# Low parts of the mixers' weight pieces: all on VectorE, in place of VectorE and GpSimd in turns

## The chip, the core and the metric

The kernel runs on one core of a Trainium2 chip. The metric is the device time of one execution in microseconds, the median of several runs. All times inside the execution come from one run that was taken with the hardware profiler; they count from the start of that run's span.

## What is computed

One layer of a streaming encoder on a sequence of 512 frames of width 1024, in float32:

```python
x = x + 0.5 * swiglu(rms_norm(x, norm_ffn1), gate1, up1, down1)     # D_FF = 2816
p = rms_norm(x, norm_mix) @ w_in
q, k, v, rw = split(p)                                              # two mixers share one projection
o_sb = rms_norm(stick_breaking_attention(q, k, v))                  # 8 heads of 64, causal
o_rw = rwkv7_time_mix(rw, ...)                                      # 8 heads, a recurrence over 512 steps
x = x + concat(o_sb, o_rw) @ w_out
x = x + 0.5 * swiglu(rms_norm(x, norm_ffn2), gate2, up2, down2)
```

The mixers are the three middle lines of work: the input projection, the attention, the recurrence and the output projection.

## The kernel before, in words

The kernel has three stages: the first feed-forward layer (to about 355 us), the mixers (to about 755 us) and the second feed-forward layer. Every weight is read once from HBM, in pieces of 128 x 512 floats.

**How a piece is made ready.** A float32 product is built from three faster ones: each operand is written as a high part plus a low part, and `mm3` (L183) issues high x high, high x low and low x high into one PSUM bank. `load` (L155) takes one of three `raw` slots and puts a load of 256 KB on SP's queue. `w_split` (L160) then has two steps: ScalarE copies the piece, rounded, into the high part (L163), and the engine handed in as `pool` subtracts, low = raw - high (L164). The high and the low part have three slots each as well. A `raw` slot comes free when L164 has read it, so L164 also sets when the load three pieces on can start.

**Which engine subtracts.** `load_split` (L167) chooses it. Outside the mixers it is VectorE. A flag is set before the mixers and cleared after them, and while it is set a counter sends the odd pieces to GpSimd:

```python
wct[0] += 1
pool = nc.gpsimd if mixing[0] and wct[0] % 2 else nc.vector
```

The mixers have 76 such pieces: 28 of `wrw` (keys, receptances, values and small factors of the recurrence) and 16 of `wqk`, all called `w` in the trace, 16 of `wv` (for `sv`, the attention's values) and 16 of `wo` (the output projection). In turns, that is 38 for each engine.

**What else VectorE and GpSimd do there.** VectorE empties PSUM banks, builds the operands of the recurrence (`item_r`, L598 to L627: `AR` at L608 to L610, `kkn` at L621, two quarters of `BK` at L625), runs a forward substitution of 15 short steps (`G` and `H`, L706 and L708), sums the attention's scores (`l` and `r`, L871 to L873) and adds the output projection into `x` (L917). GpSimd makes the other two quarters of `BK` (L625), a few masks and identities, and the sum of squares of the two inner norms (L219). It cannot read PSUM.

**What sets the order.** The program is written out flat. A loop by hand at the end of the mixers deals out three kinds of side work (the substitution and block inverse `I`, the chain of states `C`, the attention `T`) between the steps of the dense stream, by a table of costs, and gives `I` and `C` a higher priority. From these priorities, the dependencies and the free slots the framework's scheduler fixes, when the program is built, one order of instructions for each engine, by durations of its own for each engine and operation. At run time each engine works down its own list; an instruction that has to wait holds up all that stand behind it. Which engine an instruction is put on is an input of that scheduler, so a change of engine can also change the order elsewhere.

Of the kernel before, what the change touches and what calls it, by code (L numbers as in the profile page):

```python
# [82 lines left out]
def layer(ctx, tc, a, out, dbg=None):  # L83
    nc = tc.nc
# [3 lines left out]
    pd = ctx.enter_context(tc.tile_pool(name="pd", bufs=1, space=bass.MemoryType.DRAM))  # L88
    pp = ctx.enter_context(tc.tile_pool(name="pp", bufs=1, space=bass.MemoryType.PSUM))
    uid = [0]  # L90
    mixing = [False]

    def nm(s):
        uid[0] += 1
# [7 lines left out]
    def slot(tag, s="t", dt=F32, shape=None):  # L102
        return pb.tile(shape or [P, T], dt, tag="s" + tag, name=nm(s), bufs=NB[tag])
# [46 lines left out]
        return cst[:, CST[n][0]:CST[n][1]]  # L150


    wct = [0]

    def load(src, n, s="w"):  # L155
        raw = pw.tile([P, T], F32, tag="raw", name=nm(s), bufs=NW)
        nc.sync.dma_start(raw[:, :n], src)
        return raw

    def w_split(raw, n=T, s="w", pool=nc.vector, cp=nc.scalar.copy):  # L160
        hi = pw.tile([P, T], F32R, tag="whi", name=nm(s + "h"), bufs=NW)
        lo = pw.tile([P, T], F32R, tag="wlo", name=nm(s + "l"), bufs=NW)
        cp(hi[:, :n], raw[:, :n])  # L163
        pool.tensor_tensor(lo[:, :n], raw[:, :n], hi[:, :n].bitcast(F32), SUB)  # L164
        return hi, lo

    def load_split(src, n, s="w", pool=None, cp=nc.scalar.copy):  # L167
        if pool is None:
            wct[0] += 1
            pool = nc.gpsimd if mixing[0] and wct[0] % 2 else nc.vector  # L170
        return w_split(load(src, n, s), n, s, pool, cp)

    mms = []
# [69 lines left out]
    def gemm(ps, wsrc, xs, step=lambda: None):  # L243

        n = len(xs)
        for k0 in range(0, n, 4):
            kn = min(4, n - k0)
            wh, wl = load_split(wsrc[:, k0 * P:(k0 + kn) * P], kn * P)
            for k in range(k0, k0 + kn):
                ks = slice((k - k0) * P, (k - k0 + 1) * P)  # L250
                mm3(ps, wh[:, ks], wl[:, ks], xs[k][0], xs[k][1], k == 0, k == n - 1)
            step()
# [113 lines left out]
    def ffn(g, wgu, wd, last):  # L366
# [4 lines left out]
        if last:  # L371
            xsrc = pd.tile([KD, P, T], F32, name="xmid")
            for k in range(KD):
                nc.sync.dma_start(xsrc[k], X[k])
            xs = norm_in(g, XTAG)
            first = None
        else:
            xs = []

            def first():  # L380

                ps = [bank(("acc", "ma")[q], "gu"[q]) for q in range(2)]
                z = slot("f", "warm", BF16)
                nc.vector.memset(z, 0.0)
                for _ in range(11):
                    nc.tensor.matmul(ps[1], lhsT=z[:, 0:P], rhs=z, start=True, stop=True)
                for k in range(KD):
                    if k:
                        nc.sync.dma_start(X[k], a["xT"][k])
                    if k % 4 == 0:  # L390
                        w = [load_split(wgu[q][:, k * P:(k + 4) * P], T, pool=nc.vector,
                                        cp=nc.scalar.copy if k or q else nc.vector.tensor_copy) for q in range(2)]
                    xs.append(split(X[k], XTAG[k], v(g, k), "x"))
                    ks = slice(k % 4 * P, (k % 4 + 1) * P)
                    for q in range(2):
                        mm3(ps[q], w[q][0][:, ks], w[q][1][:, ks], xs[k][0], xs[k][1], k == 0, k == KD - 1)
                nc.sync.dma_start(cst, a["cst"])
                nc.sync.dma_start(lev, a["lev"])
                return ps
# [90 lines left out]
        return  # L490


    mixing[0] = True
    w2a2 = slot("g", "w2a2")
    nc.sync.dma_start(w2a2, a["w2a2"])
    g2 = slot("f", "g2")
# [327 lines left out]
    def item_sv(half):  # L824
        ps2 = [bank("acc", "sv") for _ in range(2)]
        for k in range(KD):
            wh, wl = load_split(a["wv"][k], T, "wv")
            for i in range(2):
                ts_ = slice((2 * half + i) * P, (2 * half + i + 1) * P)
                mm3(ps2[i], xs[k][0][:, ts_], xs[k][1][:, ts_], wh, wl, k == 0, k == KD - 1)  # L830
        yield
        for i in range(2):
            tt = 2 * half + i
            Vt.append(slot("v", "Vt"))
            act(Vt[tt], ps2[i], AF.Copy, scale=rs[:, tt:tt + 1])
# [147 lines left out]
    if dbg == "mix":  # L983
        return

    mixing[0] = False
    wct[0] = 0
    ffn("nf2", a["wgu2"], a["wd2"], True)


# [38 lines left out]
def build(d, dbg=None):  # L1029
    import concourse.bacc as bacc  # L1030
    nc = bacc.Bacc("TRN2", target_bir_lowering=False, num_devices=1)
    a = {n: nc.dram_tensor(n, x.shape, mybir.dt.from_np(x.dtype), kind="ExternalInput").ap() for n, x in d.items()}
    out = nc.dram_tensor("out", (KD, P, T), F32, kind="ExternalOutput").ap()
    with tile.TileContext(nc) as tc, ExitStack() as ctx:
        layer(ctx, tc, a, out, dbg)
    return nc
# [9 lines left out]
```

## Time and profile before

| what | value |
|---|---|
| median of 3 runs | 1126.36 us (1126.17 to 1126.9) |
| the profiled execution's own time | 1128.58 us |
| its span (first to last instruction) | 1126.8 us |
| TensorE (PE) busy | 1093.4 us, 97% |
| VectorE (DVE) busy | 722.2 us, 64% |
| ScalarE (ACT) busy | 522.1 us, 46% |
| GpSimd (POOL) busy | 130.1 us, 12% |
| chain that ended last | PE 78%, DVE 14%, ACT 3%, POOL 1% |

The profile names engines PE, PEld (weight loads of PE), DVE, ACT, POOL and SP. An instruction is given with its line, its operation, the tile it writes and those it reads. "Idle before" is the time for which the engine had nothing running before an instruction, with what ended it. PEclk is the clock granted to TensorE as a share of full speed; it has two levels, 2.4 GHz (1.0) and 1.2 GHz (0.5), and a value between is a mean over the stretch.

### The profile page before, as it was taken

What the parts mean: (1) busy time and instruction counts of PE and PEld (TensorE: products, weight loads), DVE (VectorE), ACT (ScalarE), POOL (GpSimd) and SP (SyncE); (2) the same over time, 40 slices, a digit from 0 to 9 for tenths busy, and PEclk for the clock granted to TensorE, in tenths of its full rate; (3) what the DMA queues carried; (4) which work ended last, traced back from release to release, by engine and by line L of the source; (5) the groups of instructions that cost most, each with busy time, mean ns of one, the idle gap of its engine ahead of it and who ended that gap; (6) DMA issues with size and microseconds to landing.
All of it is one profiled execution on the core that took longest, in us unless ns stands there. A gap on an engine that the chain in (4) does not pass through costs nothing.

```text
span 1126.8 us, 18892 instructions
## 1 busy us (share of the span) xinstructions
PE 1093.4 (97%) x7363; PEld 899.4 (80%) x7363; DVE 722.2 (64%) x1258; ACT 522.1 (46%) x958; POOL 130.1 (12%) x99
## 2 busy tenths in 40 slices
PE   8989999999999999999999998998999999999998
PEld 6789999998888766766667675676889999998887
DVE  6997777763333466477776768577987777753322
ACT  5554545542323563464644644544555454532221
POOL 0100000000003233221311302023100000000000
PEclk9999999999999998999999899999999999999999
DMA  6333333343333223311302112034333333343342
GB/s 196 102 111 96 104 111 105 103 136 96 102 96 95 95 66 108 93 47 35 82 20 57 41 24 57 11 111 131 95 122 100 90 102 113 94 143 114 113 115 67
DMA packets 70698, 104.24 MB, mean 93 GB/s; under 512 B 19664, under 2 KB 21840, under 8 KB 70608
## 3 DMA queue, kind: packets, MB, share of 16 engines
q1 hardware_dynamic: 70608, 103.02, 30.9%
q8 instruction: 58, 0.95, 0.4%
q14 instruction: 32, 0.26, 0.1%
HBM read 97.23 MB, written 5.77 MB: 91 GB/s over the span
## 4 chain that ended last, share of the span: by engine, by line
PE 78%; DVE 14%; ACT 3%; issue 2%; DMA 2%; POOL 1%; SPq 0%; DVEq 0%; ACTq 0%; POOLq 0%
PE dn L185 7%; PE dn L184 7%; PE dn L186 7%; PE pa L184 4%; PE pa L186 4%; PE pa L185 4%; PE inv L736 3%; PE g L186 2%; PE g L185 2%; PE g L184 2%; PE pc L186 2%; PE pc L185 2%; PE pc L184 2%; PE u L186 2%; PE u L185 2%
## 5 line engine op out<-in xcount | busy, mean ns | idle before, releaser
L164 DVE TENSOR_TENSOR wl<-w,wh 128x512 fp32r<-128x512 f32 x198 | 135.6, 685 | 196.0 <-ACT wh L163 194.6
L163 ACT CAST wh<-w 128x512 fp32r<-128x512 f32 (+1 forms) x219 | 132.2, 604 | 239.9 <-PE dn L185 153.6
L184 PE MATMUL dn<-hdh,wh 128*128 128x512 f32 x240 | 93.4, 389 | 0.0
L185 PE MATMUL dn<-hdl,wh 128*128 128x512 f32 x240 | 93.4, 389 | 0.0
L186 PE MATMUL dn<-hdh,wl 128*128 128x512 f32 x240 | 93.4, 389 | 0.0
L186 PEld LDWEIGHTS dn<-hdh,wl 128*128 128x128 f32 x240 | 45.1, 188 | 9.4
L184 PEld LDWEIGHTS dn<-hdh,wh 128*128 128x128 f32 x240 | 45.1, 188 | 9.3
L185 PEld LDWEIGHTS dn<-hdl,wh 128*128 128x128 f32 x240 | 45.1, 188 | 9.2
L163 ACT CAST wh<-wg 128x512 fp32r<-128x512 f32 x48 | 29.7, 620 | 38.0 <-PE u L185 21.0
L164 POOL TENSOR_TENSOR wl<-w,wh 128x512 fp32r<-128x512 f32 x22 | 31.2, 1420 | 129.6 <-ACT wh L163 107.5
L184 PE MATMUL dn<-hd,wh 128*128 128x512 f32 x112 | 43.6, 389 | 0.0
L185 PE MATMUL dn<-hd,wh 128*128 128x512 f32 x112 | 43.6, 389 | 0.0
L186 PE MATMUL dn<-hd,wl 128*128 128x512 f32 x112 | 43.6, 389 | 0.0
L186 PE MATMUL u<-xnh,wl 128*128 128x512 f32 x96 | 37.5, 390 | 0.9 <-DVE wl L164 0.9
L184 PE MATMUL g<-xnh,wh 128*128 128x512 f32 x96 | 37.6, 391 | 0.0
L185 PE MATMUL g<-xnl,wh 128*128 128x512 f32 x96 | 37.5, 391 | 0.0
L184 PE MATMUL u<-xnh,wh 128*128 128x512 f32 x96 | 37.5, 390 | 0.0
L185 PE MATMUL u<-xnl,wh 128*128 128x512 f32 x96 | 37.5, 390 | 0.0
L186 PE MATMUL g<-xnh,wl 128*128 128x512 f32 x96 | 37.5, 390 | 0.0
L164 DVE TENSOR_TENSOR wl<-wg,wh 128x512 fp32r<-128x512 f32 x48 | 33.0, 687 | 5.3 <-ACT wh L163 5.3
L318 ACT CAST s3h<-s 128x512 fp32r<-128x512 f32 x24 | 14.9, 620 | 41.3 <-DVE s L316 41.3
L219 POOL TENSOR_TENSOR sq<-sq,sq 128x512 f32<-128x512 f32 x12 | 18.0, 1500 | 111.3 <-ACT sq L135 110.6
(358 smaller groups left out, 3263.8 us busy)
## 6 DMA issues: line engine op xcount, KB each, us to landing
w<-wgu SPq DMA_DIRECT2D x80, 256.0 KB, 2.9
w<-wd SPq DMA_DIRECT2D x80, 256.0 KB, 2.6
wu<-wgu SPq DMA_DIRECT2D x48, 256.0 KB, 2.9
wg<-wgu SPq DMA_DIRECT2D x48, 256.0 KB, 2.5
w<-wrw SPq DMA_DIRECT2D x28, 256.0 KB, 2.8
x<-xT SPq DMA_DIRECT2D x16, 256.0 KB, 5.3
w<-wqk SPq DMA_DIRECT2D x16, 256.0 KB, 2.9
wv<-wv SPq DMA_DIRECT2D x16, 256.0 KB, 2.6
```

Source lines behind the costliest of these rows:

```text
L163: cp(hi[:, :n], raw[:, :n])
L164: pool.tensor_tensor(lo[:, :n], raw[:, :n], hi[:, :n].bitcast(F32), SUB)
L184: mms.append(nc.tensor.matmul(ps, lhsT=lh, rhs=rh, start=start, stop=False, skip_group_check=again))
L185: nc.tensor.matmul(ps, lhsT=lh, rhs=rl, start=False, stop=False, skip_group_check=again)
L186: nc.tensor.matmul(ps, lhsT=ll, rhs=rh, start=False, stop=stop, skip_group_check=again)
L219: (eng if k < KD - 1 else nc.vector).tensor_tensor(tot, tot, sq, ADD)
L318: nc.scalar.copy(hi, t_)
L736: nc.tensor.matmul(ps[rows[p], cc], lhsT=l_[rows[p], cc], rhs=r[rows[p], cc], start=True, stop=True)
```

## The change

In the mixers every low part is made by VectorE. The flag and the counter go, and the choice in `load_split` is always VectorE; nothing else is edited. The other work of GpSimd stays where it is.

```diff
-    mixing = [False]
...
-    wct = [0]
...
     def load_split(src, n, s="w", pool=None, cp=nc.scalar.copy):
         if pool is None:
-            wct[0] += 1
-            pool = nc.gpsimd if mixing[0] and wct[0] % 2 else nc.vector
+            pool = nc.vector
         return w_split(load(src, n, s), n, s, pool, cp)
...
-    mixing[0] = True
     w2a2 = slot("g", "w2a2")
...
-    mixing[0] = False
-    wct[0] = 0
     ffn("nf2", a["wgu2"], a["wd2"], True)
```

## Rows read from the trace of the kernel before

**Rows 1.** Busy time, page: us, share of the span, instructions.
```profile
PE 1093.4 (97%) x7363; PEld 899.4 (80%) x7363; DVE 722.2 (64%) x1258; ACT 522.1 (46%) x958; POOL 130.1 (12%) x99
```

**Rows 2.** Windows: stretch, length, busy of PE, PEld, DVE, ACT, POOL, PEclk, DMA, GB/s.
```profile
360.00:755.00 395.00, 378.23 (x3292) 273.17 (x3291) 262.76 (x495) 199.67 (x376) 94.58 (x74) 0.98 0.22 58
415.00:430.00 15.00, 11.32 (x54) 8.32 (x54) 11.35 (x13) 4.34 (x8) 6.89 (x6) 0.79 0.34 102
430.00:440.00 10.00, 10.00 (x113) 7.77 (x112) 3.53 (x9) 4.80 (x9) 3.95 (x5) 0.97 0.34 87
500.00:510.00 10.00, 9.67 (x73) 5.64 (x71) 9.59 (x12) 6.89 (x15) 5.30 (x4) 1.00 0.09 26
675.00:690.00 15.00, 12.63 (x54) 7.83 (x52) 13.40 (x28) 9.46 (x19) 1.30 (x1) 0.89 0.17 33
```

**Rows 3.** Waits in the mixers: waiter, releaser, us in all, times, longest.
```profile
DVE AR L768 <- PE MG L766: 18.1, 6, 6.9
...
PE wo L184 <- DVE x L917: 3.3, 2, 1.8
...
PE A L659 <- DVE BK L625: 2.7, 2, 1.8
```

**Rows 4.** Groups by line, GpSimd's low parts: count, busy us, mean ns, idle before.
```profile
L164 POOL TENSOR_TENSOR wl<-w,wh 128x512 fp32r<-128x512 f32 x22 | 31.2, 1420 | 129.6 <-ACT wh L163 107.5 <-PE q L186 8.9 <-DMA G<-db 6.9
...
L164 POOL TENSOR_TENSOR wvl<-wv,wvh 128x512 fp32r<-128x512 f32 x8 | 11.4, 1428 | 24.6 <-ACT wvh L163 16.2 <-DVE rn L851 8.2
L164 POOL TENSOR_TENSOR wol<-wo,woh 128x512 fp32r<-128x512 f32 x8 | 10.3, 1286 | 79.2 <-ACT woh L163 71.1 <-DVE H L708 8.1
```

**Rows 5.** Timeline of VectorE: start us, duration us, instruction, idle before it.
```profile
367.77 0.83 DVE L200 SCALAR_TENSOR_TENSOR xl<-x,vec,xh 128x512 fp32r<-128x512 f32 x1 [0.80 <-ACT xh L135]
...
416.57 1.78 DVE L610 TENSOR_TENSOR AR<-xr,Pd 128x512 f32<-128x512 f32 x1
418.27 1.76 DVE L621 TENSOR_TENSOR kkn<-kkn,a 128x512 f32<-128x512 f32 x1
...
422.31 1.75 DVE L625 TENSOR_TENSOR BK<-kkn,Pi 64x512 f32<-64x512 f32 x1
423.99 0.67 DVE L625 TENSOR_TENSOR BK<-kf,Pi 64x512 f32<-64x512 f32 x1
424.59 0.67 DVE L164 TENSOR_TENSOR wvl<-wv,wvh 128x512 fp32r<-128x512 f32 x1
...
442.19 1.16 DVE L706 TENSOR_TENSOR G<-G,H 64x25 f32<-64x25 f32 x1
...
504.77 0.68 DVE L608 SCALAR_TENSOR_TENSOR AR<-kkn,Pd 128x504 f32<-128x504 f32 x1 [0.41 <-ACT Pd L135]
...
735.18 1.42 DVE L197 TENSOR_TENSOR orl<-orw,orh 128x512 fp32r<-128x512 f32 x1 [0.24 <-ACT orh L196]
```

**Rows 6.** Timeline of GpSimd, the same columns.
```profile
417.88 1.61 POOL L164 TENSOR_TENSOR wvl<-wv,wvh 128x512 fp32r<-128x512 f32 x1
420.18 1.66 POOL L625 TENSOR_TENSOR BK<-kkn,Pi 64x512 f32<-64x512 f32 x1 [0.69 <-DVE kkn L621]
421.92 1.60 POOL L164 TENSOR_TENSOR wvl<-wv,wvh 128x512 fp32r<-128x512 f32 x1
...
501.15 1.29 POOL L164 TENSOR_TENSOR wl<-w,wh 128x512 fp32r<-128x512 f32 x1 [11.14 <-ACT wh L163]
```

**Rows 7.** Timeline of TensorE, the same columns.
```profile
419.54 0.50 PE L185 MATMUL sv<-wvl,xh 128*128 128x512 f32 x1 [0.66 <-POOL wvl L164]
...
422.44 0.50 PE L185 MATMUL sv<-wvl,xh 128*128 128x512 f32 x1 [1.25 <-DVE wvl L164]
424.72 0.59 PE L659 MATMUL A<-AR,BK 64*128 64x128 f32 x2 [1.77 <-DVE BK L625]
...
449.45 0.50 PE L185 MATMUL sv<-wvl,xh 128*128 128x512 f32 x1 [0.91 <-DVE wvl L164]
...
680.86 1.10 PE L209 MATMUL qm<-rn,cst 128*128 128x512 f32 x2 [0.53 <-DVE rn L848]
```

## The prediction

> **What bounds the kernel now.** I read the busy times first, then a table by windows, then who waited for whom in the mixers, then the groups by line, and last the timelines of three engines side by side. By the busy times TensorE works for 97% of the span [rows 1]. In the mixers, 360 to 755 us, it is busy for 378.23 of 395 us at a mean clock of 0.98 [rows 2]: 16.8 us stand idle there, and about 8 us (395 x 0.02) are lost to the lower clock. No change on VectorE and GpSimd can win more than these two. VectorE is busy for 262.76 us there, 67% on the mean, but 9.59 of 10 us from 500 to 510 [rows 2]; TensorE's longest waits are for VectorE, those for `x` and `BK` [rows 3] among them, in stretches where VectorE itself has no pause. So the question is what the change does to VectorE in those few stretches, not to the mean. (A measurement of this kernel tells about 0.2%, 2.25 us, from no change.)
>
> **What goes and what comes.** GpSimd loses 22 + 8 + 8 = 38 subtractions with means of 1.29 to 1.43 us [rows 4]. VectorE gets them. The undisturbed one at 424.59 lasts 0.67 us, but its predecessor, just as long, started 0.60 us before it [rows 5], so each takes 0.60 us of VectorE's list: 38 x 0.60 = 22.8 us.
>
> Part of that comes back. While GpSimd runs, a VectorE instruction with two inputs stands still: `kkn` at 418.27 takes 1.76 us beside GpSimd's `wvl` of 417.88, and `BK` at 422.31 takes 1.75 us beside that of 421.92, while the next `BK` takes 0.67 us alone [rows 5, 6]. That is 1.08 us each. Even the tiny `G` step of 25 columns at 442.19 takes 1.16 us [rows 5]. The timeline has 18 VectorE instructions stretched by a low part of GpSimd, the first at 367.77, the last at 735.18 [rows 5]; what they take beyond undisturbed ones of their kind adds up to 11.7 us. VectorE's list thus grows by 22.8 - 11.7 = 11.1 us, from 67 to about 69% of the mixers. The Trainium skill (SBUF — State Buffer, Who interferes with whom) says that the two engines share a pair of ports under an exclusive lock, and that the loser blocks for the whole instruction. If each of the 38 met such an instruction, by that rule, 38 x 1.29 = 49 us would come back, VectorE would get lighter and the loss below would go: the sum would be -3.5 us in place of -2.0. The trace shows the block, but for 18 of 38.
>
> **Place by place.** A moved instruction counts where TensorE's next idle time is ended by VectorE or by the low part itself.
>
> *415 to 425 us.* TensorE waits 0.66, 1.25 and 1.77 us [rows 7], for GpSimd's `wvl`, for VectorE's `wvl` and for `BK`. `AR` at 416.57 [rows 5] waited for GpSimd's own `BK`, which stays. Then the first moved `wvl` runs on VectorE from 418.3 to 418.9, where GpSimd ended it at 419.49 (417.88 + 1.61) [rows 6]: TensorE goes on 0.5 us sooner. `kkn` loses a stall of 1.08 us for an added 0.60 us: 0.5 us. GpSimd's `BK` of 420.18 [rows 6] and VectorE's `wvl` behind it move up with it. The second moved `wvl` replaces the stall of `BK` at 422.31: another 0.5 us. `A` starts 1.0 us sooner: **-1.0**, and 2.7 of the 3.68 us of idle time stay.
>
> *The clock there.* It is 0.79 over 15 us and 0.97 over the next 10 [rows 2]: 15 x 0.21 + 10 x 0.03 = 3.45 us lost. From 675 to 690 us TensorE waited 0.53 us [rows 7] and then 1.8 us for `x` [rows 3], 2.3 us in all, and lost 15 x 0.11 = 1.65 us [rows 2]. With 2.7 us of idle time left the first place comes near the second, so I take 1.65 us for the loss that remains: **-1.8**. Ends: 0, if the fall stays as it is, and -3.45, if it goes.
>
> *438 to 450 us.* Three moved `wvl` add 1.8 us ahead of the one that ends the 0.91 us wait at 449.45 [rows 7]; three stalls of `G` steps (the one shown and two more) give back 2.2 us: **-0.4**.
>
> *690 to 702 us.* Two moved `wol` add 1.2 us, two stretched sums give back 1.6 us, ahead of one of the two waits for `x` [rows 3]. Some of it ends in waits for ScalarE: **-0.3**.
>
> *500 to 635 us.* Five moved instructions (like the one at 501.15 [rows 6]) stand in full stretches of VectorE ahead of waits of TensorE for `BK`, `Z`, states and scores, and no VectorE instruction is stretched by them today. Each costs between 0 us, where a pause as the 0.41 us at 504.77 [rows 5] swallows it, and 0.60 us. I take half: **+1.5**.
>
> *The other 26.* I cost them at nothing: after them TensorE has work in its list, and the pieces stand up to three ahead. The 38 that VectorE makes today show that this cover is thick: TensorE waited for a low part only in the `sv` stages. If the cover went, each would cost 0.60 us less its share of the remaining stalls (11.7 - 2.2 - 2.2 - 1.6 = 5.7 us): 26 x 0.60 - 5.7, some +10 us.
>
> *Queues.* SP's list is the same: 76 loads in the same places of the program. Their slots come free at the subtraction, on GpSimd after its 1.29 us, on VectorE after 0.67 us and whatever stands ahead. What stands ahead can be long: VectorE waits 6.9 us once for a product `MG` [rows 3], and a low part behind that would hold its load as well. On GpSimd the `BK` quarters and masks only get freer.
>
> **Sum.** -1.0 - 1.8 - 0.4 - 0.3 + 1.5 = -2.0 us. The profiled execution took 1128.58 us (span 1126.8) and would take 1126.6; it stands 2.2 us above the median of the runs, so the forecast goes on the median: 1126.36 - 2.0 = **1124.4 us**. Its own range, with the ends of the clock and of the five (0 to +3.0): 1121.2 (-1.7 - 3.45 + 0) to 1127.7 (-1.7 + 0 + 3.0).
>
> **The rivals.** *VectorE becomes the bound in its full stretches* (500 to 520 and 556 to 640 us). For it: 9.59 of 10 us busy [rows 2] with a pause of 0.41 us [rows 5] before the operands of `A`. Price: eight moved instructions there without a stall, 8 x 0.60 = 4.8 us, one more fall of the clock like that at 675 us, 1.65 us, and of the gains only the -1.0 and -0.7 stay: +4.7, about **1131**. It decides once the pauses before `AR` and `Z` are used up, that is when 0.60 us exceeds the 0.41. Against it: in these stretches ScalarE or TensorE ended some of VectorE's pauses, so part is swallowed. The Trainium skill (Perfetto Trace Analysis, Optimizing Scalar/DVE Operations) stands on this side: with VectorE saturated, handing some of its work to GpSimd may pay, though the shared port may eat that up. The trace bears out both halves, the full 10 us and the 18 stalls.
>
> *The places link up.* With the stalls gone at 415 to 425 us the clock doesn't fall there (-3.45) and the five are swallowed (0): -1.7 - 3.45 = -5.2, **1121.2**. For it: if the second moved `wvl` is put behind the `BK` pair in VectorE's list, another 0.60 us goes, and 2.1 us of idle time stay, less than the 2.3 us of the second place. Against: that order is not known.
>
> *It is hidden.* TensorE is busy 378 of 395 us; what is won in one pause is waited for in the next. **1126.4**.
>
> That the change doesn't do what it says I leave out: one argument decides the engine. But the scheduler orders all lists anew, and a shift of a few us either way through other neighbours is in the range.
>
> **How the numbers follow.** Forecast 0.40, places linked 0.22, hidden 0.10, VectorE the bound 0.28. Of the forecast's own range, 1121.2 to 1127.7, I put 0.17 of the 0.40 below 1124.1, the rest within 0.2%. Faster 0.22 + 0.17 = 0.39; same 0.23 + 0.10 = 0.33; slower 0.28. The range for 8 in 10 reaches from below the linked case, 1118.5, to just above the slower one, 1131.5; outside lie the lost cover (+10) and luck of the order.
>
> **What would show it.** GpSimd's busy time falls by 53 us to about 77, with no line of low parts; VectorE's rises by some 14 (38 x 0.67 - 11.7). `kkn` and the first `BK` at 415 to 425 us take 0.67 us; TensorE's waits there add up to 2.7 us or less and the clock of 415 to 430 us is near 0.89. Wrong would be: waits of TensorE for `BK`, `Z` or `x` longer by 0.6 us each, a fall of the clock at a new place, or TensorE waiting for low parts in `k`, `r`, `q` or `wo`.

## The result, and the profile after

The changed kernel takes **1121.83 us** (median of 6 runs, 1120.58 to 1122.28) beside 1127.82 us for the kernel before (6 runs, 1126.17 to 1130.95): a ratio of **0.995, interval 0.9931 to 0.9968**. Run again later it gave 0.9968 (0.9953 to 0.9983). It is faster, by 3.6 to 5.6 us where 2.0 were forecast. The experiments below show that most of this is not the work of the engine that the change names: with the order held, putting the 38 subtractions on VectorE changes the time by -1.4 to +1.9 us (ratios that are each uncertain by about 2 us), while the new order that the scheduler gave the lists wins 4.3 to 4.4 us by itself.

The page of the changed kernel (its profiled execution took 1122.11 us, its span is 1120.3 us; lines stand 2 to 4 lower than before):

```profile
PE 1090.7 (97%) x7363; PEld 896.7 (80%) x7363; DVE 727.5 (65%) x1296; ACT 520.6 (46%) x958; POOL 79.3 (7%) x61
```

GpSimd lost 50.8 us and 38 instructions against [rows 1]; VectorE has the 38 more, and yet is busy for 5.3 us more only. The windows, with the columns of [rows 2]:

```profile
360.00:755.00 395.00, 382.12 (x3319) 275.27 (x3319) 275.11 (x543) 204.39 (x386) 48.42 (x40) 1.00 0.23 63
415.00:430.00 15.00, 12.84 (x86) 9.60 (x86) 11.81 (x20) 5.20 (x10) 3.10 (x2) 1.00 0.48 137
430.00:440.00 10.00, 10.00 (x98) 8.04 (x97) 5.38 (x18) 6.03 (x11) 3.76 (x4) 1.00 0.35 95
500.00:510.00 10.00, 9.07 (x60) 6.25 (x55) 9.60 (x13) 6.96 (x14) 3.95 (x2) 1.00 0.01 2
510.00:580.00 70.00, 68.33 (x732) 49.11 (x731) 47.33 (x104) 33.33 (x69) 8.47 (x8) 1.00 0.19 51
675.00:690.00 15.00, 11.39 (x46) 7.22 (x44) 13.39 (x31) 7.37 (x21) 0.00 (x0) 0.89 0.24 50
```

In the mixers TensorE is busy for 382.12 of 395 us in place of 378.23, and the mean clock rounds to 1.00 in place of 0.98. The window 415 to 430 us runs at full clock, 675 to 690 us does not. One window that I had not read before the change is the most telling later on; the same 510 to 580 us of the kernel before:

```profile
510.00:580.00 70.00, 65.90 (x665) 47.37 (x667) 48.20 (x102) 36.55 (x74) 15.53 (x13) 1.00 0.19 51
```

TensorE's waits in the mixers of the changed kernel (waiter, releaser, us in all, times, longest):

```profile
PE z L857 <- DVE rn L847: 3.3, 1, 3.3
PE wT L876 <- DVE r L869: 2.9, 6, 0.9
PE inv L732 <- DVE Z L738: 2.0, 4, 0.7
PE sv L182 <- DVE wvl L162: 1.5, 1, 1.5
PE A L655 <- DVE BA L658: 0.5, 1, 0.5
...
PE wo L181 <- DVE x L913: 0.4, 2, 0.3
```

TensorE's two waits of [rows 3] changed: `wo` waits for `x` for 0.4 us, not 3.3, and `A` for `BK` not at all, where it was 2.7. A new one came, 3.3 us of `z` for `rn` at 675 to 679 us, and the one fall of the clock that is left in the mixers (680.0 to 683.4 us) stands behind it. Before, the granted clock fell to its lower level from 423.8 to 430.7, 635.5 to 642.3 and 686.7 to 690.1 us. The last product of the mixers ends at 756.4 us, not 763.4: all of the gain lies in the mixers, and they start within 0.1 us of each other.

At the first place of the prediction, VectorE, GpSimd and TensorE (columns of [rows 5]):

```profile
415.71 0.68 DVE L617 TENSOR_TENSOR kkn<-kkn,a 128x512 f32<-128x512 f32 x1
416.31 0.68 DVE L162 TENSOR_TENSOR wvl<-wv,wvh 128x512 fp32r<-128x512 f32 x1
416.92 1.78 DVE L607 SCALAR_TENSOR_TENSOR xr<-xr,vec,kf 128x512 f32<-128x512 f32 x1
418.62 2.35 DVE L162 TENSOR_TENSOR wvl<-wv,wvh 128x512 fp32r<-128x512 f32 x2
420.90 0.67 DVE L621 TENSOR_TENSOR BK<-kkn,Pi 64x512 f32<-64x512 f32 x1
421.50 0.67 DVE L621 TENSOR_TENSOR BK<-kf,Pi 64x512 f32<-64x512 f32 x1
...
416.73 1.42 POOL L621 TENSOR_TENSOR BK<-kf,Pi 64x512 f32<-64x512 f32 x1 [2.02 <-ACT Pi L134]
418.11 1.72 POOL L621 TENSOR_TENSOR BK<-kkn,Pi 64x512 f32<-64x512 f32 x1
...
420.43 0.50 PE L182 MATMUL sv<-wvl,xh 128*128 128x512 f32 x1 [1.47 <-DVE wvl L162]
...
425.30 1.79 PE L655 MATMUL A<-AR,BK 64*128 64x128 f32 x16 [0.55 <-DVE BA L658]
```

`kkn` and both `BK` take 0.67 to 0.68 us as forecast. GpSimd's own `BK`, which stayed, now blocks `xr` (1.78 us) and the first of two low parts. The neighbours are others than in [rows 5], since the low parts stand at other places of the list. By the two traces, TensorE's list is the same for its first 2229 products, up to 412.3 us in the `sv` stage, and ScalarE's up to 413.6 us. VectorE's list, its low parts left aside, is the same up to 463 us and differs behind that.

### The profile page after: what moved, and what is told of

Same layout as the page of the kernel before. It is cut to its first block, busy times and chain, and to the rows that moved or that the text cites. A ratio compares the mean times of both kernels' runs of the same rounds, so it can differ in the third digit from the quotient of the medians.

```text
span 1120.3 us, 18878 instructions
## 1 busy us (share of the span) xinstructions
PE 1090.7 (97%) x7363; PEld 896.7 (80%) x7363; DVE 727.5 (65%) x1296; ACT 520.6 (46%) x958; POOL 79.3 (7%) x61
## 4 chain that ended last, share of the span: by engine, by line
PE 78%; DVE 13%; ACT 3%; issue 2%; POOL 1%; DMA 1%; SPq 0%; DVEq 0%; ACTq 0%; POOLq 0%
PE dn L183 7%; PE dn L182 7%; PE dn L181 7%; PE pa L181 4%; PE pa L183 4%; PE pa L182 4%; PE g L182 2%; PE g L181 2%; PE g L183 2%; PE pc L183 2%; PE pc L182 2%; PE pc L181 2%; PE u L181 2%; PE u L183 2%; PE u L182 2%
## 5 line engine op out<-in xcount | busy, mean ns | idle before, releaser
L162 DVE TENSOR_TENSOR wl<-w,wh 128x512 fp32r<-128x512 f32 x220 | 151.0, 687 | 200.6 <-ACT wh L161 199.4
L181 PE MATMUL pa<-xch,s2h 128*128 128x256 f32 x96 | 27.4, 285 | 3.5 <-ACT cu L332 3.5
L134 ACT ACTIVATE l<-l 128x128 f32<-128x128 f32 (+3 forms) x64 | 28.8, 467 | 0.9
```

Source lines behind the costliest of these rows:

```text
L134: ins = nc.scalar.activation(out_, in_, func, **kw)
L181: mms.append(nc.tensor.matmul(ps, lhsT=lh, rhs=rh, start=start, stop=False, skip_group_check=again))
```

## The experiments

Three theories stood against each other. **Work** (A in the expectations): the relieved GpSimd no longer blocks VectorE, and that is the gain. **Order** (B): the gain is the scheduler's new order, whichever engine subtracts. **Both needed**: the new order pays only without the blocked port. To hold the order while the engine changes, every instruction was listed in the wanted order, and each was tied to the one before it on its engine by a dependency that only fixes the order and adds no wait:

```python
for i in range(0, len(raw), 2):
    at += int.from_bytes(raw[i:i + 2], "little", signed=True)
    ins = insts[at]
    e = str(ins.engine)
    if e in last:
        tc.add_manual_dep(ins, last[e],
                          mybir.DependencyInfo(mybir.DependencyClass.NoSync, mybir.DependencyReason.DATA),
                          reason="order")
    last[e] = ins.name
```

Here `raw` holds the wanted order. The traces show that it was held: TensorE's 7363 products, ScalarE's 958 instructions, the loads, and VectorE's 972 instructions other than these low parts stand in the order of the kernel that was to lend it.

Ratios are to the kernel before on the same chip, 6 or 12 runs each.

**All on VectorE, in the order of before** (twice). The edit is the change itself and the lines above with the order of before.

> All low parts on VectorE, but every engine keeps the order of the kernel before; a moved low part stands in VectorE's list where it stood in the scheduler's common list. Theory A (GpSimd's low parts cost time themselves: they stop VectorE, 11.7 us in 18 places, and last 1.3 us in place of 0.7): most of the gain is here, 4 to 6 us faster than before, both clock falls at 424 and 635 us gone or shorter. Theory B (the gain comes from the new order of the lists, the engine alone is worth little): within 2 us of before, the clock falls stay.

> All low parts on VectorE in the order of before throughout, once more, as the common base of these runs: ratio 0.9997 to 1.004 if the division of work alone wins nothing (the first time it was 1.0017); at most 0.998 if that first time was an unlucky chip or moment and the relieved GpSimd is what makes the changed kernel faster.

Measured: 1129.17 us, ratio 1.0017 (0.9997 to 1.0037), and 1126.88 us, ratio 1.0011 (0.9993 to 1.0029); the medians of the kernel before on these chips are 1128.73 and 1126.97 us. No gain without the new order. Windows of the second, then TensorE's longest waits in its mixers:

```profile
360.00:755.00 395.00, 376.00 (x3294) 271.46 (x3293) 274.62 (x535) 200.90 (x378) 40.22 (x37) 0.99 0.22 59
415.00:430.00 15.00, 12.28 (x60) 9.23 (x59) 11.38 (x17) 4.04 (x7) 3.28 (x3) 0.77 0.32 92
...
510.00:580.00 70.00, 65.97 (x675) 47.37 (x671) 49.10 (x104) 35.70 (x73) 8.46 (x8) 1.00 0.20 51
```

```profile
PE wo L181 <- DVE x L913: 3.4, 2, 1.9
PE inv L732 <- DVE Z L738: 3.3, 2, 1.7
PE wT L876 <- DVE r L869: 2.7, 5, 1.2
PE A L655 <- DVE BK L621: 2.2, 2, 1.3
PE sv L182 <- DVE wvl L162: 1.6, 2, 1.3
```

Every wait of [rows 3] is nearly where it was, the clock at 415 to 430 us is 0.77 in place of 0.79, and TensorE is busy for 65.97 us from 510 to 580, in place of 65.90. Not all falls of the clock stay: those at 635 and 686 us are missing here, and one at 699 us is new.

**In turns as before, in the order of the changed kernel** (twice). The edit is the kernel before and the lines above.

> Low parts in turns as before, but every engine keeps the order of the changed kernel. Theory A: the gain is gone, within 2 us of before or slower, with VectorE instructions of 1.1 to 1.8 us beside GpSimd's low parts. Theory B: the gain is kept, 4 to 6 us faster than before.

> VectorE and GpSimd in turns, in the changed kernel's order throughout, once more: 0.995 to 0.998 if the order makes the gain whichever engine subtracts (the first time it was 0.9962); 1.000 or more if it takes the relieved GpSimd too.

Measured: 1123.49 us, ratio 0.9962 (0.9947 to 0.9978), and 1123.1 us, ratio 0.9961 (0.9944 to 0.9979). GpSimd makes its 38 low parts as before, they still stretch some 17 VectorE instructions by 13 to 14 us in all, and the gain is there all the same. Windows of the second:

```profile
360.00:755.00 395.00, 379.15 (x3308) 272.91 (x3306) 262.33 (x502) 202.89 (x383) 96.95 (x76) 1.00 0.22 61
415.00:430.00 15.00, 11.85 (x82) 8.79 (x82) 11.06 (x15) 4.06 (x8) 7.68 (x5) 1.00 0.39 119
...
510.00:580.00 70.00, 68.41 (x729) 48.76 (x728) 45.99 (x98) 33.92 (x70) 15.07 (x13) 1.00 0.19 51
```

The row of 510 to 580 us sorts the kernels by order and not by engine: 68.3 to 68.4 us busy in the new order, 65.0 to 66.0 in the old one (65.0 in the first run with all on VectorE). Put together:

| low parts made | order of before | order of the changed kernel |
|---|---|---|
| in turns | 1 | 0.9962, 0.9961 |
| all on VectorE | 1.0017, 1.0011 | 0.995, 0.9968 |

Down a column the engine changes: +1.2 to +1.9 us in the old order (0.0011 and 0.0017 of 1126), -1.4 to +0.8 us in the new one. The intervals in the old order hold 1, those in the new one overlap: no difference is shown, and one of about 2 us either way is not excluded. Along a row the order changes: -4.3 and -4.4 us above, -4.8 to -7.5 us below (extremes of the ratios). Order is the theory that stands.

The profiles leave something open for the engine. From the end of the first feed-forward layer to the end of the output projection, the two of the changed kernel take 390.1 and 390.8 us with 12.9 and 13.8 us of TensorE idle; the two in turns in the same order take 393.7 and 393.0 us with 14.3 and 15.9 us idle. In the old order it is the other way round in idle time: 16.8 us in turns, 18.6 and 19.1 us with all on VectorE. So the new order may go a little better with a relieved GpSimd; the medians of the runs don't show it.

**The changed kernel, again.** No edit.

> The changed kernel itself, beside the next three on one chip, as their common measure. Ratio to before 0.993 to 0.997, as it was.

Measured: 1122.27 us, ratio 0.9968 (0.9953 to 0.9983), on the chip of the next two and of the sums further down.

**Where the order gains: half of one order, half of the other.** All on VectorE, the orders joined at a point: three kernels take the new order up to the point and the old one behind it, one the reverse.

> All low parts on VectorE; the order of the changed kernel until the last product of the sv stages (about 450 us), the order of the kernel before after that. Old order throughout was at 1.0017 of before, new order throughout at 0.995. Theory B1 (the order gains in the sv stages, where three waits of TensorE and a fall of the clock stand before): ratio 0.997 or less. Theory B2 (it gains in the later inverses, at the waits for Z, BK and x): 1.000 or more.

> The same, with the new order until the last N product of the second inverse (about 580 us) and the old order after it. B1: as new_to_sv, 0.997 or less. B2: if the gain lies in the second inverse (BK and Z at 510 and 568 us), 1 to 3 us below new_to_sv; if it lies in the third and fourth (635 to 720 us), as new_to_sv, 1.000 or more.

> All low parts on VectorE; every engine in the changed kernel's order up to the last product N of the second block inverse (at about 580 us), in the order of before behind it. If the gain of the new order is made between 450 and 580 us: ratio at most 0.998 to the kernel before, and TensorE's idle time in the mixers up to there as in the changed kernel. If it is made behind 580 us (other neighbours at 635 and 686 us, no fall of the clock there): ratio 0.9995 to 1.003, with the clock's falls at 635 and 686 us back.

> The reverse: the order of before up to 580 us, the changed kernel's order behind it, all low parts on VectorE. If the gain is made behind 580 us: ratio at most 0.998, the fall of the clock near 425 us stays and those at 635 and 686 us are gone. If it is made ahead of 580 us: ratio 0.9995 to 1.003. If it needs both: this one and the one above both lie within 0.9985 and 1.0015.

Measured: 0.9992 (0.9978 to 1.0005) with the point behind the last `sv` product at about 450 us; 0.9999 (0.9979 to 1.0019) for the next, whose point was misplaced: it fell into the first block inverse at about 475 us, not into the second, so it says little more than the one before; 1.0008 (0.999 to 1.0026) with the new order up to 580 us; 1.0027 (1.001 to 1.0043) with the old order up to there. None keeps the gain, and the reverse one is even a little slower. That is neither "ahead of 580 us" nor "behind it". The kernel with the new order up to 580 us does have the fuller window (68.06 us of 510 to 580) and no fall of the clock at 424 us, but behind the point TensorE waits:

```profile
580.37 0.33 PE L785 MATMUL S<-St,AR 64*64 64x64 f32 x4 [0.64 <-DVE St L771]
583.40 1.79 PE L655 MATMUL A<-AR,BK 64*128 64x128 f32 x10 [1.83 <-DVE St L786]
```

These two are 2.5 us at the joint, the clock falls there (583.7 to 587.1 us), and falls again at 634.9 and 699.7 us. A joined order has a joint of its own that neither whole order has, so these four runs don't place the gain: which moves of the new order carry it **stays open**.

**In turns, but the even pieces on GpSimd**, in whatever order the scheduler gives.

```diff
-            pool = nc.gpsimd if mixing[0] and wct[0] % 2 else nc.vector
+            pool = nc.gpsimd if mixing[0] and wct[0] % 2 == 0 else nc.vector
```

> In turns, but the even pieces on GpSimd and the odd ones on VectorE; the scheduler orders the lists anew. It shows what a new order is worth without a change in the division of work. Theory A: within 2 us of before. Theory B: it can differ from before by as much as the change did, 3 us or more, either way.

Measured: 1129.15 us, ratio 1.0005 (0.9988 to 1.0022). The same share of work and a third order, without a gain; TensorE stands idle for 22.8 us in its mixers, where it is 16.8 before and 12.9 in the changed kernel, and the clock falls six times there. So a new order is not better by being new; the one that the change drew was a good one.

**GpSimd reads along.** The changed kernel in its own order; GpSimd gets an instruction of two inputs back for each odd piece, whose output nobody reads. The edit against the kernel before, without the lines that tie the order (`tc.extra` keeps the added instructions out of them):

```diff
-            pool = nc.gpsimd if mixing[0] and wct[0] % 2 else nc.vector
-        return w_split(load(src, n, s), n, s, pool, cp)
+            pool = nc.vector
+        r = w_split(load(src, n, s), n, s, pool, cp)
+        if mixing[0] and wct[0] % 2:
+            idle = pw.tile([P, 480], BF16, tag="idle", name=nm("idle"), bufs=1)
+            x = r[0][:, :480].bitcast(F32)
+            tc.extra.append(nc.gpsimd.tensor_tensor(idle, x, x, SUB).ins.name)
+        return r
```

> The changed kernel in its own order, and beside each low part that GpSimd made before, GpSimd subtracts the high part from itself into a tile that nobody reads (480 columns, about 1.2 us); nothing waits for it. Theory A, its part on the stops of VectorE: 3 to 5 us slower than the changed kernel. If only the length of the low parts or the order counts: within 1 us of the changed kernel.

Measured: 1140.88 us, ratio 1.0121 (1.0101 to 1.0141), by the ratios 17 to 19 us above the changed kernel, and only part of it is what the run was made for. In the mixers the extra reads stretch some 28 VectorE instructions by about 16 us in all, TensorE's idle time rises from 12.9 to 18.2 us, and the clock spends 6.8 us more at its lower level. The mixers are 11.4 us longer. But the first feed-forward layer is 3.3 us longer and the second 3.8, where GpSimd has no extra work (up to 1.7 us of the 3.3 are a fall of the clock near 72 us, 3.4 us long, that the other profile lacks). There the same products last longer. The groups of one product between 800 and 1100 us, in the changed kernel and in this one (busy us, mean ns):

```profile
L181 PE MATMUL dn<-hdh,wh 128*128 128x512 f32 x104 | 40.5, 389 | 0.0
```

```profile
L190 PE MATMUL dn<-hdh,wh 128*128 128x512 f32 x85 | 33.6, 396 | 0.0
```

396 ns against 389, at the same granted clock of 1.00; from start to start it is 233 against 227 ns. The chip is not the reason: the three other kernels of this section that ran on it (both orders, and the even pieces on GpSimd) have 227 ns. The other difference of the two kernels is the added tile, which takes 960 bytes of every partition and may shift the tiles behind it. I didn't try a kernel with the tile and without the reads, so why the products lengthen is open, and the price of the blocked port is at most what the mixers show: 5.3 us of idle time and up to 3.4 us of clock. A small part of that is another wait: an added read holds its high part, and ScalarE waits once for one, 1.1 us. The waits that it lengthened:

```profile
PE inv L742 <- DVE Z L748: 4.0, 4, 2.3
PE z L867 <- DVE rn L857: 3.3, 1, 3.3
PE wT L886 <- DVE r L879: 3.3, 4, 2.1
PE sv L191 <- DVE wvl L165: 1.9, 2, 1.6
PE A L665 <- DVE BK L631: 1.7, 1, 1.7
```

`inv` for `Z` is 4.0 us, not 2.0, and `A` waits for `BK` again. Fifteen of the stretched instructions, all but one of 511 or 512 columns, end 0.55 us after the end of the added read beside them: VectorE does its work behind the read. That bears out the rule that the prediction drew from the Trainium skill (SBUF — State Buffer, Who interferes with whom): the loser of the shared port stands for the whole instruction. It suggests, too, why the change alone is worth so little: what the blocking costs is won only if VectorE doesn't take the blocker's work in exchange.

**The sums of squares of the second feed-forward layer, too.** GpSimd's other long work at a place where TensorE waits.

```diff
-                S, _, _ = norm_scale(eng=nc.vector if first else nc.gpsimd)
+                S, _, _ = norm_scale(eng=nc.vector)
```

> The changed kernel with the six sums of squares of the second feed-forward layer's norm on VectorE too. GpSimd makes them from 749 to 760 us and five instructions of VectorE beside them take 0.4 to 1.1 us more, on the way from the mixers' last product to the second feed-forward layer, where TensorE waits 1.0 and 1.9 us. Theory A for this place (the stops on the path cost time): 2 to 3 us faster than the changed kernel. Rival (six added VectorE instructions stand ahead of what TensorE waits for, or the new order eats it): within 1 us or slower.

Measured: 1117.69 us, ratio 0.9919 (0.9899 to 0.9938), 4.6 us below the changed kernel on the same chip (1122.27). Behind the mixers, the waits of TensorE in the changed kernel, then in this one:

```profile
758.25 0.49 PE L181 MATMUL u<-xh,wh 128*128 128x512 f32 x1 [0.99 <-ACT wh L161]
760.91 0.50 PE L183 MATMUL g<-xh,wl 128*128 128x512 f32 x1 [1.94 <-DVE wl L162]
```

```profile
756.92 0.50 PE L181 MATMUL u<-xh,wh 128*128 128x512 f32 x1 [1.11 <-DVE xl L197]
```

The wait of 1.94 us for a low part on VectorE is gone, and so is the fall of the clock from 761.9 to 765.3 us; the mixers end as before (754.9 us; 755.1 in the changed kernel on that chip), and what follows takes 360.1 in place of 363.1 us. This kernel beats both. Its lists, too, were ordered anew (TensorE's list differs from about 763 us of its trace on), so how much of it is the engine and how much the order was not tried.

## Why the prediction was right, and where it was not

The time fell into the range and on the forecast side, but that was luck: the sum is worked out for the old order of the lists, and with that order the runs gained nothing (1.0017 and 1.0011, where -2.0 us would be 0.9982). There it can be held against the rows step by step (the second run in that order).

- *415 to 425 us, -1.0.* Right: the waits there are 1.29 and 1.29 us, 2.6 in all, where 2.7 were to stay.
- *The clock there, -1.8, ends 0 and -3.45.* **This step failed.** "With 2.7 us of idle time left the first place comes near the second": in the old order the idle time shrank as forecast and the fall stayed whole in both runs' profiles, 426.2 to 433.0 us in the first and 422.6 to 429.5 us in the second, where it is 0.77 over the window. With GpSimd still in turns but in the new order there are 3.0 us of idle time (2.45 and 0.58) and in one of two profiles no fall at all. The sum of the idle time at the place does not order these cases; of the two ends that were given, 0 was the value.
- *438 to 450 us, -0.4.* Right: the 0.91 us wait is 0.29, and of that 0.3 us go to the wait for `Vt` right behind it (0.38 in place of 0.08): -0.3.
- *690 to 702 us, -0.3.* The two waits for `x` are 3.4 us, not 3.3. Nothing came of it.
- *500 to 635 us, +1.5, ends 0 and +3.0.* Right within its ends, above its middle: the waits for operands of `A`, `Z`, states and scores between 500 and 636 us add up to 8.6 us (0.54, 0.90, 0.69, 1.01, 1.67, 0.99, 1.17 and 1.63) against 6.2 (0.97, 0.69, 0.33, 1.66, 0.38, 0.73 and 1.48): +2.4.
- *The other 26, nothing.* Right: no wait for a low part in `k`, `r`, `q` or `wo`.
- *VectorE's busy time, +14.* In the old order 733.0 us, +10.8. Held against the median of undisturbed instructions of the same shape, the 18 stretches of the kernel before add up to some 14 us, not 11.7, which is most of the difference. The +5.3 of the changed kernel is the new order's: in turns in that order VectorE is at 717.1 us, 5.1 below before.

With the clock at 0 the steps give -1.0 - 0.4 - 0.3 + 1.5 = -0.2 us; with the measured sizes -1.1 - 0.3 + 0.1 + 2.4 = +1.1; the ratios of the runs in the old order say +1.2 and +1.9, with intervals that hold 0. So the division of work is a trade of equals: the runs here can't tell the two divisions apart. The Trainium skill (Perfetto Trace Analysis, Optimizing Scalar/DVE Operations) says of handing work from VectorE to GpSimd that it might not help, since the two share a port; these runs agree (1.0017 and 1.0011).

Why only 18 of the 38 met a stretch can be read more closely than the prediction did. It spoke of VectorE instructions with two inputs. In the kernel before, `xru`, a product of two inputs of which one lies in PSUM, runs undisturbed beside GpSimd's low part of 501.15 [rows 6], and a copy with one input, 0.36 to 0.38 us long at other places, is stretched beside the low part of 613.05:

```profile
501.19 0.67 DVE L523 TENSOR_TENSOR xru<-r,S 128x512 f32<-128x512 f32 x1
```

```profile
613.39 1.17 DVE L709 COPY H<-H 64x256 f32<-64x256 f32 x1
```

So the number of inputs does not sort them.

The other fault is what I did with the order. That "a shift of a few us either way through other neighbours is in the range" treated it as luck around a sum; it is the main term. Its size was visible beforehand only as a bound: 16.8 us of idle time and 8 us of clock. The changed kernel has 3.9 us less of idle time and spends 13.7 us less at the lower clock (3.4 in place of 17.1). The mixers got 7.1 us shorter, so by these two profiles the 13.7 us had cost 3.2 us, and not the half of their length that the sum counted for such time. The rival *the places link up* named the right number, 1121.2, by the wrong road: its gain was to come from the stalls, and the stalls may stay. *VectorE becomes the bound* came half true in the old order, +2.4 of its 4.8 us. (Its eight moved instructions without a stall are five by the trace, at 501.15, 518.46, 557.50, 586.06 and 606.73 us; those at 613.05 and 621.18 stretch a VectorE instruction. Five would be 3.0 us.) *It is hidden* is the case nearest to what the change of engine does by itself.

How an order can win a wait is seen at one place. Before, VectorE's `AR` of the second block of the recurrence stands behind six steps of the attention's scores and three shifts, and ScalarE's `Pd`, for which it waits last, is late likewise: it starts at 504.77 [rows 5], and what hangs on it ends late:

```profile
510.02 0.67 DVE L625 TENSOR_TENSOR BK<-kf,Pi 64x512 f32<-64x512 f32 x1
...
510.75 1.16 PE L659 MATMUL A<-AR,BK 64*128 64x128 f32 x16 [0.97 <-DVE BK L625]
```

In the changed kernel `AR` stands ahead of most of the scores:

```profile
498.76 0.68 DVE L604 SCALAR_TENSOR_TENSOR AR<-kkn,Pd 128x504 f32<-128x504 f32 x1
...
500.68 0.68 DVE L606 TENSOR_TENSOR AR<-xr,Pd 128x512 f32<-128x512 f32 x1
...
507.68 0.67 DVE L621 TENSOR_TENSOR BK<-kkn,Pi 64x512 f32<-64x512 f32 x1
508.27 0.67 DVE L621 TENSOR_TENSOR BK<-kf,Pi 64x512 f32<-64x512 f32 x1
...
509.78 1.16 PE L655 MATMUL A<-AR,BK 64*128 64x128 f32 x16
```

VectorE is as full as before from 500 to 510 us (9.60 and 9.59 of 10 us), `BK` ends at 508.9, and `A` at 509.78 waits for nothing. The scores pay for it with a wait of 0.91 us of `wT` at 505.5. In the old order with all low parts on VectorE, `A` waits 0.90 us here, as before.

## What to carry to other kernels

Where a scheduler orders the lists from engines and costs, changing one instruction's engine changes two things; measure them apart by tying the lists to one order, or the credit goes to the wrong one. A helper that blocks the main engine for 1.08 us and saves it 0.60 us of work, but meets it only 18 times in 38, was a trade of equals here: look for work that can leave both. And a forecast for such an edit needs the order as a term of its own, bounded by TensorE's idle time and lower clock in the stage.

## What the runs showed that was not expected

- The products of 128 x 512 lasted 396 ns in place of 389 in all stages of one kernel, 233 in place of 227 ns from start to start, at the same granted clock. The three other kernels on that chip had 227 ns. What it is due to was not tried; besides the added reads, an added tile is the only edit.
- The falls of the clock are not fixed by the program: with the same code ahead of them, one execution in the old order shows a fall near 71 us and the other none, and two executions of the kernel with turns in the new order show one near 422 us and none. Executions of one kernel lie up to 10 us apart (1126.68 to 1136.56, all on VectorE in the old order), so for differences like these only medians of several runs count.
